# A one-layer transformer trunk in split float32: the gates of three paired blocks put behind the copies of their last sums, two embedding splits put behind the last pair's, and every queue ordered by the scheduler's timeline model

## The chip, the cores and the metric

The kernel runs on one core of a Trainium2 chip. The metric is the device time of one execution in microseconds (us). Three executions of the kernel before took 662.04, 662.87 and 664.4 us; the median, 662.87 us, is what the change is measured against. The profile shown below is of one further execution, which took 664.42 us.

A core has five engines that work side by side, each through a queue of its own in strict order: TensorE (PE, matmuls), VectorE (DVE), ScalarE (ACT), GpSimd (POOL) and SyncE (SP), which here issues nearly all transfers from memory. They wait for one another by semaphores. An instruction whose data is not there yet holds up everything behind it on its engine.

## The reference

The layer is an attention mixer, a layer norm, a gated MLP with a causal convolution, a second layer norm, and a gated embedding. Sequence 512, width 1024, 16 heads of 64, inner width 2816, all in float32:

```python
proj = x @ w_in                                  # q, k, v, f_logit
c = cumsum(log_sigmoid(f_logit + b_f))           # per head
s = q @ k.T * scale + c[:, None] - c[None, :]    # causal
o = softmax(s) @ v
x = layer_norm(ALPHA * x + o @ w_out, ln_mix_g, ln_mix_b)
u, g = split(x @ ffn_w_up)
g = causal_dwconv(g, conv_w, conv_b)             # 3 taps
x = layer_norm(ALPHA * x + (gelu(g) * u) @ ffn_w_down, ln_ffn_g, ln_ffn_b)
x = x + sigmoid(x @ ple_w_gate + ple_b_gate) * (p @ ple_w_proj)
```

## The kernel before

**Split products.** A float32 product is made of three matmuls in a faster format. Each operand is split into a high part (`xh`, `whi`), which ACT makes by a copy, and a low part (`xl`, `wlo`), which DVE makes by subtracting the high part from the original. `three` (L120) issues hi x hi, hi x lo and lo x hi into one PSUM bank. A matmul over 512 columns is the kernel's unit of work.

**Weights** come in units of 1024 columns (`Weights`): SP loads a unit into one of four buffers `raw`, ACT writes `whi` (L98), DVE writes `wlo` (L99), and a matmul reads both. Units are numbered in the order of use; `whi25` is the high part of unit 25. A unit's `home` gives it a tile of its own rather than one of the rotating five; only the embedding's splits (`moreh`, `morel`) have one.

**Stages.** Values (`pv`); then, for each of the 16 heads, projections for a pair of heads further on (`pp`, 24 matmuls each), scores (`s6_0` to `s6_3` are the four row blocks of head 6), softmax (DVE adds the mask, L404, and takes the negated maximum, L405; ACT takes the exponential with its sum, L406; POOL scales by the reciprocal, L414), ten transposes (`t`, L427) into three banks that ACT and DVE copy as high and low parts (`PTh`, L430, `PTl`, L431), and the product with the values (`o`, L440). The scores of a head are issued a head ahead of its transposes and two ahead of its values. Then the output projection (`ao` and `ap`, for the left and right 512 columns), the first layer norm, whose result is transposed back by PE (`nt`, L558) and split, the MLP's up products (`g` gate, `u` up) and down products (`x`, `y`, `z`), the last down products (`r`), the second layer norm, the embedding's product (`pl`), its gate (`gt`), and the output.

**A layer norm** here (`add_half`, `half_stats`, `norm`) costs DVE for each of four row tiles: two adds of a product (L533 or L535), two statistics (L540), an aggregate (L544), an addition (L545), then two passes over 1024 columns (L549 and L550), between which POOL raises to a power (L546). `flip` transposes the finished tile.

**Up pairs.** The inner blocks are worked in pairs. For pairs 4, 7 and 9 (`UP_PAIRS`) a scheme with fewer products is used, in four stages of sums (`up_step`); the sums end in `E4`, `E7` and `E9`. The last stage ends with a copy of a bank into E by ACT (L697). Then `conv_product` takes the gate through the convolution and Gelu (`conv`, `product`). Down products of the group of pairs before are issued in between, wherever `between()` stands.

**What sets the order.** The kernel is written in one thread; a scheduler (`TileContext`) places each instruction in its engine's queue by the priority that it had when written and by what is ready in the scheduler's own model. `BANKS` deals out the eight PSUM banks in turn. A new user of a bank waits for the last reader of the old one.

Of the kernel before, what the change touches and what calls it, by code (L numbers as in the profile page):

```python
# [12 lines left out]
AF = mybir.ActivationFunctionType  # L13
# [3 lines left out]
P = 128  # L17
S = 512
# [16 lines left out]
HALF = S // 2  # L35
# [21 lines left out]
class Weights:  # L57

    def __init__(self, nc, pool):
        self.nc, self.pool = nc, pool
        self.units, self.raw, self.parts = [], {}, {}
        self.loaded = self.cut = 0

# [19 lines left out]
    def cut_to(self, i):  # L85
        while self.cut < min(i, len(self.units)):
            self.load_to(self.cut + 1)
            _, n, _, make, home = self.units[self.cut]
            t = self.raw.pop(self.cut)
            if home is not None:  # L90
                hi, lo = home()
            else:
                hi, lo = [self.pool.tile([P, UNIT], F32R, tag=g, name=f"{g}{self.cut}", bufs=SPLIT_BUFS)
                          for g in ("whi", "wlo")]
            c = 0
            for piece in [t[:, :n]] if make is None else make(t):
                e = c + piece.shape[-1]
                self.nc.scalar.activation(hi[:, c:e], piece, AF.Copy)  # L98
                self.nc.vector.tensor_sub(lo[:, c:e], piece, hi[:, c:e].bitcast(F32))  # L99
                c = e  # L100
            self.parts[self.cut] = (hi, lo)
            self.cut += 1

# [7 lines left out]
def trunk_layer(ctx: ExitStack, tc: tile.TileContext, xT, x2d, pT, wqk, wv0, wv1, wv2, bf, wo, wup, cwb,  # L111
                wdn, wpl, wg, bg, gm, bm, gf, bff, out):
    nc = tc.nc
# [9 lines left out]
    base = ctx.enter_context(tc.tile_pool(name="base", bufs=1))  # L123
# [8 lines left out]
    def half_rows(w, k0, n, cols):  # L132
        return w[k0 * P:(k0 + n) * P, cols * 512:(cols + 1) * 512].rearrange("(k p) c -> p k c", p=P)

    W = Weights(nc, base)
    wv = (wv0, wv1, wv2)
    u_v, u_qk = {}, []

# [79 lines left out]
    for part in range(4):  # L218
# [3 lines left out]
        for i in range(2 * len(fs)):  # L222
            f, q = fs[i // 2], i % 2
# [13 lines left out]
                    u_up[j, 3, sq] = stages[3](sq)  # L237
        assert not todo
    u_r = [[W.add(half_rows(wdn, k, 2, n), inner=512) for k in REST[::2]] for n in range(2)]
    extra = []  # L240

    def apart(i):
        return lambda: [t[:, i] for t in extra]

    u_p = W.add(pT.rearrange("(k p) t -> p k t", p=P), inner=S, home=apart(0))
    u_pl = [W.add(half_rows(wpl, 0, 2, n), inner=512, home=apart(1 + n)) for n in range(2)]
# [410 lines left out]
    def up_step(j, st, s, E):  # L657

        if st == 0:
            ups[j, s] = bank(f"{'gu'[s]}{2 * j}", "two" if j > 2 else None)
        ps = ups[j, s]
        z, x = ps[:, :HALF], ps[:, HALF:]
        hi, lo = W.get(u_up[j, st, s], 2)
        first, second = slice(0, HALF), slice(HALF, S)

        def go(to, col, on, a=None, sn=None, last=4):
            for k in range(4):
                w = slice((4 * col + k) * P, (4 * col + k + 1) * P)  # L670
                if a is None:
                    mh, ml = [v[:, 4 * sn + k, :] for v in xs]
                else:
                    mh, ml = [v[:, a[0] + k, a[1]] for v in (x1h, x1l)]
                three(to, hi[:, w], lo[:, w], mh, ml, k == 0 and not on, k == 3, on=on)

        e = E[:, (1 - s) * 2 * S:(2 - s) * 2 * S]
        c1, c2 = side(5)[:, s * HALF:(s + 1) * HALF], side(6 + s)
        if st == 0:
            go(z, 1, False, a=(4, first))  # L680
            go(x, 0, True, a=(0, first))
            nc.scalar.activation(c1, z, AF.Copy)
            nc.scalar.activation(z.rearrange("p (a b) -> p a b", b=P),
                                 zeros.unsqueeze(1).to_broadcast([P, 2, P]), AF.Copy)
            nc.vector.tensor_add(e[:, :HALF], x, c1)
        elif st == 1:
            go(z, 0, True, sn=0)
            go(x, 1, True, sn=1)
            nc.scalar.activation(c2[:, :HALF], x, AF.Copy)
            nc.scalar.activation(c2[:, HALF:], z, AF.Copy)  # L690
        elif st == 2:
            go(z, 1, True, sn=3)
            go(x, 0, True, sn=2)
            nc.vector.tensor_add(e[:, S:], ps, c2)  # L694
        else:
            go(x, 0, True, a=(4, second))
            nc.scalar.activation(e[:, HALF:S], x, AF.Copy)  # L697
            del ups[j, s]

    def conv_product(f, E):  # L700

        c = slice(f % 2 * S, f % 2 * S + S)
        ups[f, 0], ups[f, 1] = E[:, 2 * S:][:, c], E[:, c]
        conv(f)
        product(f, E[:, c])
# [61 lines left out]
    for part in range(4):  # L767
        ops = []
        slots = iter(CHUNKS[part] or ())

        def between():
            for _ in range(next(slots, 0)):
                next(before)

        for f in range(6 * part, min(6 * part + 6, NF)):
            q, j = f % 2, f // 2
            if q == 0:
                E = hpool.tile([P, 8 * HALF], F32, tag="E", name=f"E{j}")
            if f == 0:
                a, b = slice(0, HALF), slice(HALF, S)  # L780
                up(0, 0, a)
                up(0, 1, a)
                up(1, 0, a, (3, x1h, x1l, xt))
                up(0, 0, b)
                up(0, 1, b)
                up(1, 0, b)
                conv(0)
                product(0, E[:, :S])
                continue
            if j in UP_PAIRS:  # L790
                if q == 0:
                    up_step(j, 0, 0, E)
                    between()
                    up_step(j, 0, 1, E)
                    between()
                    continue
                for st in (1, 2):
                    up_step(j, st, 0, E)
                    up_step(j, st, 1, E)
                    if st == 1:  # L800
                        between()
                conv_product(f, E)
                between()
                up_step(j, 3, 0, E)
                up_step(j, 3, 1, E)
                conv_product(f - 1, E)
            else:
                if f > 1:
                    up(f, 0)
                conv(f)  # L810
                between()
                up(f, 1)
                product(f, E[:, q * S:(q + 1) * S])
            if f == 1:
                x_sums()
            if q:
                if part < 3:
                    ops.append([cut_tiles("A", 2, 3, f"a{j}"), cut_tiles("B", 1, 5, f"b{j}", pool=hpool),
                                cut_tiles("S", 4, 4, f"s{j}")])
                    operands(ops[-1], E)  # L820
                else:
                    h, l = cut_tiles("S", 4, 4, f"s{j}")
                    e = E[:, :2 * S].rearrange("p (a b) -> p a b", b=HALF)
                    nc.scalar.activation(h, e, AF.Copy)
                    nc.vector.tensor_sub(l, e, h.bitcast(F32))
                    ops.append((h, l))
            if j not in UP_PAIRS:
                between()
        if part < 3:
            before = down(part, ops)  # L830
# [126 lines left out]
```

## Time and profile before

| | |
|---|---|
| three executions | 662.04, 662.87, 664.4 us |
| profiled execution | 664.42 us |
| its span (first to last instruction) | 662.7 us |
| PE busy | 650.9 us (98%) |
| DVE busy | 514.3 us (78%) |
| ACT busy | 339.2 us (51%) |
| POOL busy | 84.3 us (13%) |
| TensorE clock granted, mean | 0.996 |

Busy times of the engines overlap and are not to be added. In the rows of the timeline the columns are start, duration, engine, line, operation, result and sources, and how many instructions of that kind follow each other; in square brackets stands the idle time of the engine before the row and what ended it. Consecutive instructions of one engine overlap a little in these records (a DVE instruction starts some 0.08 us before the end of the one before it, a copy on ACT some 0.1 us), so a row of durations adds up to a little more than the time it takes.

### The profile page before, as it was taken

The page shows a single profiled execution, that of the slowest core. Times are in us where ns is not written, and L with a number is a line of the kernel's source. Part 1 is how long each engine was busy: PE and PEld are TensorE (multiplying, and loading weights), DVE is VectorE, ACT ScalarE, POOL GpSimd, SP SyncE. Part 2 cuts the span into 40 slices and gives each one's busy share as a digit, 9 for nine tenths or more (in the row PEclk, how much of TensorE's full clock was granted, in tenths as well). Part 3 has the DMA queues.
Part 4 walks back from the last instruction along what each step waited for, and adds up shares of the span by engine and source line. Part 5 has one row for each costly group of instructions (what it writes and reads, how often), then busy time and mean ns, then how long its engine had stood idle before and what let it go on. Part 6 is the DMA issues. An engine that isn't in the chain of part 4 may idle for free.

```text
span 662.7 us, 9314 instructions
## 1 busy us (share of the span) xinstructions
PE 650.9 (98%) x3450; PEld 563.4 (85%) x3450; DVE 514.3 (78%) x830; ACT 339.2 (51%) x589; POOL 84.3 (13%) x78
## 2 busy tenths in 40 slices
PE   8999999999999999999999999999999989999997
PEld 7899888888888889888889888889888978788886
DVE  7674789998886699954889696797878887599364
ACT  5644677787775255643445544354545543516231
POOL 0000554445445020000000000000000000011000
PEclk9999999999999999999999999999999989999999
DMA  8433122112262313433344554645544553651221
GB/s 291 158 129 128 64 66 66 42 57 66 65 227 107 120 43 101 133 117 95 102 139 145 181 156 146 182 131 191 185 137 126 186 157 120 203 204 64 71 79 48
DMA packets 35485, 83.29 MB, mean 126 GB/s; under 512 B 3248, under 2 KB 7088, under 8 KB 35440
## 3 DMA queue, kind: packets, MB, share of 16 engines
q1 hardware_dynamic: 35440, 82.70, 38.6%
q8 instruction: 27, 0.44, 0.3%
q14 instruction: 18, 0.15, 0.1%
HBM read 80.46 MB, written 2.10 MB: 125 GB/s over the span
## 4 chain that ended last, share of the span: by engine, by line
PE 88%; DMA 4%; DVE 4%; ACT 2%; issue 2%; SPq 0%; ACTq 0%; DVEq 0%
PE g L120 16%; PE u L120 15%; PE pp L120 13%; PE gt L120 7%; PE pv L120 6%; PE x L120 6%; PE ao L120 3%; PE ap L120 3%; PE o L440 3%; PE r L120 3%; PE z L120 3%; PE t L427 2%; DMA raw<-wdn 2%; DVE wlo L99 2%; PE pl L120 2%
## 5 line engine op out<-in xcount | busy, mean ns | idle before, releaser
L98 ACT ACTIVATE whi<-raw 128x1024 fp32r<-128x1024 f32 (+5 forms) x143 | 133.3, 934 | 136.7 <-PE g L120 44.4
L99 DVE TENSOR_TENSOR wlo<-raw,whi 128x1024 fp32r<-128x1024 f32 (+5 forms) x143 | 151.4, 1065 | 53.9 <-ACT whi L98 53.7
L414 POOL TENSOR_SCALAR pr<-pr,rl 128x128 f32<-128x128 f32 (+1 forms) x64 | 72.0, 1143 | 135.7 <-DVE rl L410 135.7
L120 PE MATMUL g<-x1h,whi 128*128 128x512 f32 (+1 forms) x180 | 64.0, 355 | 3.4 <-ACT E L697 3.4
L120 PE MATMUL g<-x1l,whi 128*128 128x512 f32 (+1 forms) x180 | 63.5, 353 | 0.0
L120 PE MATMUL g<-x1h,wlo 128*128 128x512 f32 (+1 forms) x180 | 63.4, 352 | 0.0
L120 PE MATMUL u<-x1h,whi 128*128 128x512 f32 (+1 forms) x172 | 61.5, 357 | 0.7 <-DVE E L694 0.7
L120 PE MATMUL u<-x1l,whi 128*128 128x512 f32 (+1 forms) x172 | 61.4, 357 | 0.0
L120 PE MATMUL u<-x1h,wlo 128*128 128x512 f32 (+1 forms) x172 | 61.4, 357 | 0.0
L546 POOL TENSOR_TENSOR mv<-mv,neghalf 128x1 f32<-128x1 f32 x8 | 11.6, 1447 | 386.5 <-DVE mv L545 364.2
L120 PE MATMUL pp<-xh,wlo 128*128 128x512 f32 x128 | 50.5, 395 | 0.0
L120 PE MATMUL pp<-xh,whi 128*128 128x512 f32 x128 | 50.0, 390 | 0.0
L120 PE MATMUL pp<-xl,whi 128*128 128x512 f32 x128 | 50.0, 390 | 0.0
L406 ACT ACTIVATE pr<-s,nm 128x128 f32<-128x128 f32 (+1 forms) x64 | 33.4, 526 | 17.4 <-DVE nm L405 14.3
L120 PEld LDWEIGHTS g<-x1h,whi 128*128 128x128 f32 x180 | 34.4, 191 | 8.6 <-ACT E L697 4.0
L120 PEld LDWEIGHTS g<-x1l,whi 128*128 128x128 f32 x180 | 34.4, 191 | 4.7
L120 PEld LDWEIGHTS g<-x1h,wlo 128*128 128x128 f32 x180 | 34.5, 191 | 4.6
L120 PEld LDWEIGHTS u<-x1h,whi 128*128 128x128 f32 x172 | 32.5, 189 | 5.6 <-issue 0.9
L120 PEld LDWEIGHTS u<-x1l,whi 128*128 128x128 f32 x172 | 32.5, 189 | 4.8
L120 PEld LDWEIGHTS u<-x1h,wlo 128*128 128x128 f32 x172 | 32.5, 189 | 4.7
L630 ACT ACTIVATE a<-a 128x512 f32<-128x512 f32 x22 | 13.9, 631 | 34.8 <-DVE a L628 34.8
L120 PE MATMUL pv<-whi,xh 128*128 128x384 f32 (+1 forms) x96 | 30.3, 328 | 1.0 <-ACT whi L98 1.0
(535 smaller groups left out, 1624.6 us busy)
## 6 DMA issues: line engine op xcount, KB each, us to landing
raw<-wup SPq DMA_DIRECT2D x50, 512.0 KB
raw<-wdn SPq DMA_DIRECT2D x31, 512.0 KB
raw<-wqk SPq DMA_DIRECT2D x16, 512.0 KB
raw<-wo SPq DMA_DIRECT2D x8, 512.0 KB
raw<-wg SPq DMA_DIRECT2D x8, 512.0 KB
raw<-wv SPq DMA_DIRECT2D x8, 384.0 KB
side<-wdn SPq DMA_DIRECT2D x9, 256.0 KB
raw<-wdn SPq DMA_DIRECT2D x9, 256.0 KB
```

Source lines behind the costliest of these rows:

```text
L98: self.nc.scalar.activation(hi[:, c:e], piece, AF.Copy)
L99: self.nc.vector.tensor_sub(lo[:, c:e], piece, hi[:, c:e].bitcast(F32))
L120: nc.tensor.matmul(ps, lhsT, rhs, start=start and n == 0, stop=stop and n == 2, skip_group_check=on)
L406: nc.scalar.activation(pr[:, off:off + w], ps[:, :w], AF.Exp, bias=nm[:, i:i + 1], accum_out=ls[:, i:i + 1])
L414: nc.gpsimd.tensor_scalar_mul(pr[:, off:off + w], pr[:, off:off + w], rl[:, i:i + 1])
L427: nc.tensor.transpose(ps[:, w:w + P], pr[:, o:o + P], ident)
L440: nc.tensor.matmul(ps[:, q0:], V[:, j, h], p[:, o:o + w], start=j == 0 and n == 0, stop=j == NT - 1 and n == 1)
L546: nc.gpsimd.tensor_tensor(mv[:, 3:4], mv[:, 2:3], neghalf, op=ALU.pow)
L630: nc.scalar.activation(a, a, AF.Gelu)
```

## The change

Four things are changed; no instruction is added or taken away on any engine, and no arithmetic is changed.

1. A unit with a `home` is split inside `issue_after(first)`, where `first` is the ACT copy that starts the last pair's splits (`s10h<-E10`, L824 before). The embedding's three splits (`moreh`, `morel`) so stand behind it in ACT's queue.
2. The copies and additions that end each stage of `up_step` are written under `tc.high_priority()`, and the last stage returns the ACT copy with which it ends.
3. In pairs 4, 7 and 9 both calls of `conv_product` stand after the last stage and inside `issue_after` of its copy. So the ACT work of the two gates stands behind the copy of the last sum.
4. `TileContext` is given `schedule_with_timeline_sim=True`: the scheduler orders all queues by another model of the engines' time.

```diff
             t = self.raw.pop(self.cut)
+            behind = ExitStack()
             if home is not None:
-                hi, lo = home()
+                hi, lo, first = home()
+                behind.enter_context(self.tc.issue_after(first))
...
+            behind.close()
             self.parts[self.cut] = (hi, lo)
...
-    extra = []
+    extra, last_cut = [], []
     def apart(i):
-        return lambda: [t[:, i] for t in extra]
+        return lambda: [t[:, i] for t in extra] + [last_cut[0]]
...
         if st == 0:
             go(z, 1, False, a=(4, first))
             go(x, 0, True, a=(0, first))
-            nc.scalar.activation(c1, z, AF.Copy)
-            nc.scalar.activation(z.rearrange("p (a b) -> p a b", b=P),
-                                 zeros.unsqueeze(1).to_broadcast([P, 2, P]), AF.Copy)
-            nc.vector.tensor_add(e[:, :HALF], x, c1)
+            with tc.high_priority():
+                nc.scalar.activation(c1, z, AF.Copy)
+                nc.scalar.activation(z.rearrange("p (a b) -> p a b", b=P),
+                                     zeros.unsqueeze(1).to_broadcast([P, 2, P]), AF.Copy)
+                nc.vector.tensor_add(e[:, :HALF], x, c1)
...
         else:
             go(x, 0, True, a=(4, second))
-            nc.scalar.activation(e[:, HALF:S], x, AF.Copy)
             del ups[j, s]
+            with tc.high_priority():
+                return nc.scalar.activation(e[:, HALF:S], x, AF.Copy)
...
-                conv_product(f, E)
                 between()
                 up_step(j, 3, 0, E)
-                up_step(j, 3, 1, E)
-                conv_product(f - 1, E)
+                with tc.issue_after(up_step(j, 3, 1, E).ins):
+                    conv_product(f, E)
+                    conv_product(f - 1, E)
...
-                    nc.scalar.activation(h, e, AF.Copy)
+                    last_cut[:] = [nc.scalar.activation(h, e, AF.Copy).ins]
...
-    with tile.TileContext(nc) as tc:
+    with tile.TileContext(nc, schedule_with_timeline_sim=True) as tc:
```

Parts 1 and 3 put instructions behind one that is named. Part 4 moves instructions everywhere, also in the attention and the layer norms, which parts 1 to 3 do not touch. Three places show it. In the changed file the lines stand two or three lower (L98 is L100, L431 is L434, L550 is L553).

**In the attention, at head 6.** ACT's queue from the copies of projection 3 on, before and then in the changed kernel (`t4_0`, `t4_1`, `t4_3` are the banks of head 4's transposes):

```order
L379 ACTIVATE KA6_1217<-pp3_1_1191 64x512
L380 ACTIVATE KB0_295<-pp3_1_1191 64x512
L430 ACTIVATE PTh0_299<-t4_0_1226 128x512
L430 ACTIVATE PTh0_299<-t4_1_1233 128x384
L430 ACTIVATE PTh0_299<-t4_3_1239 128x384
L379 ACTIVATE KA7_1259<-pp3_1_1191 64x512
L446 ACTIVATE o_1_1149<-o3_1245 64x512
L380 ACTIVATE KB1_296<-pp3_1_1191 64x512
L98 ACTIVATE whi25_1607<-raw25_1305 128x1024
```

```order
L382 ACTIVATE KA6_1217<-pp3_1_1191 64x512
L383 ACTIVATE KB0_295<-pp3_1_1191 64x512
L100 ACTIVATE whi25_1607<-raw25_1305 128x1024
L433 ACTIVATE PTh0_299<-t4_0_1226 128x512
L433 ACTIVATE PTh0_299<-t4_1_1233 128x384
L433 ACTIVATE PTh0_299<-t4_3_1239 128x384
L382 ACTIVATE KA7_1259<-pp3_1_1191 64x512
L383 ACTIVATE KB1_296<-pp3_1_1191 64x512
```

DVE's queue at the same place, before and then in the changed kernel:

```order
L383 TENSOR_TENSOR KA6_1217<-pp3_1_1191,KA6_1217 64x512
L431 TENSOR_TENSOR PTl0_301<-t4_0_1226,PTh0_299 128x512
L431 TENSOR_TENSOR PTl0_301<-t4_1_1233,PTh0_299 128x384
L431 TENSOR_TENSOR PTl0_301<-t4_3_1239,PTh0_299 128x384
L447 TENSOR_TENSOR o_1_1149<-o3_1245,o_1_1149 64x512
```

```order
L386 TENSOR_TENSOR KA6_1217<-pp3_1_1191,KA6_1217 64x512
L101 TENSOR_TENSOR wlo25_1608<-raw25_1305,whi25_1607 128x1024
L434 TENSOR_TENSOR PTl0_301<-t4_0_1226,PTh0_299 128x512
L407 TENSOR_TENSOR s6_0_1271<-s6_0_1271,mask_82 128x128
L407 TENSOR_TENSOR s6_1_1272<-s6_1_1272,mask_82 128x128
L434 TENSOR_TENSOR PTl0_301<-t4_1_1233,PTh0_299 128x384
L407 TENSOR_TENSOR s6_2_1277<-s6_2_1277,mask_82 128x128
L434 TENSOR_TENSOR PTl0_301<-t4_3_1239,PTh0_299 128x384
```

The two halves of the split of unit 25 have moved ahead of the copies of the transposes, and three mask additions stand between those copies.

**In the first layer norm.** DVE's queue, before and then in the changed kernel (`ap0`, `ap1`, `ap2` are the right half products of row tiles 0, 1 and 2; `mv_2505` belongs to tile 0, `mv_2538` to tile 1):

```order
L533 SCALAR_TENSOR_TENSOR y_2210<-y_2210,ap0_2454 128x512
L540 BN_STATS st0_2443<-y_2210 128x6
L544 BN_AGGR mv_2505<-st0_2443 128x2
L545 TENSOR_SCALAR mv_2505<-mv_2505 128x1
L549 SCALAR_TENSOR_TENSOR y_2210<-y_2210,mv_2505,g1_2426 128x1024
L550 SCALAR_TENSOR_TENSOR y_2210<-y_2210,mv_2505,b1_2428 128x1024
L533 SCALAR_TENSOR_TENSOR y_2210<-y_2210,ap1_2511 128x512
```

```order
L536 SCALAR_TENSOR_TENSOR y_2210<-y_2210,ap2_2544 128x512
L547 BN_AGGR mv_2538<-st1_2446 128x2
L548 TENSOR_SCALAR mv_2505<-mv_2505 128x1
L552 SCALAR_TENSOR_TENSOR y_2210<-y_2210,mv_2505,g1_2426 128x1024
L543 BN_STATS st2_2449<-y_2210 128x6
L548 TENSOR_SCALAR mv_2538<-mv_2538 128x1
L552 SCALAR_TENSOR_TENSOR y_2210<-y_2210,mv_2538,g1_2426 128x1024
L553 SCALAR_TENSOR_TENSOR y_2210<-y_2210,mv_2505,b1_2428 128x1024
```

PE's queue where the transposes of tile 0 stand, before and then in the changed kernel:

```order
L120 MATMUL ap2_2544<-whi34_2455,ol_98 128x512
L120 MATMUL ap2_2544<-wlo34_2456,oh_97 128x512
L558 MATMUL nt_2557<-ident_80,y_2210 128x128 x4
L558 MATMUL nt_2564<-ident_80,y_2210 128x128 x4
L120 MATMUL ap2_2544<-whi35_2467,oh_97 128x512
```

```order
L123 MATMUL ap2_2544<-whi36_2479,ol_98 128x512
L123 MATMUL ap2_2544<-wlo36_2480,oh_97 128x512
L561 MATMUL nt_2557<-ident_80,y_2210 128x128 x4
L561 MATMUL nt_2564<-ident_80,y_2210 128x128 x4
L123 MATMUL ap3_2593<-whi33_2371,oh_97 128x512
```

Tile 0 was finished on DVE before the product `ap1` was read; now its last pass stands seven rows behind the reading of `ap2`, and its transposes on PE follow the last matmul of `ap2` at once.

**In the second layer norm.** DVE's queue up to the last pass of the third tile (`mv_5654`), before and then in the changed kernel:

```order
L549 SCALAR_TENSOR_TENSOR y_2210<-y_2210,mv_5654,g2b2_5518 128x1024
L535 TENSOR_TENSOR y_2210<-y_2210,r1_0_5674 128x512
L550 SCALAR_TENSOR_TENSOR y_2210<-y_2210,mv_5654,g2b2_5518 128x1024
L540 BN_STATS st1_5688<-y_2210 128x6
L535 TENSOR_TENSOR y_2210<-y_2210,r1_1_5690 128x512
```

```order
L101 TENSOR_TENSOR wlo137_5807<-raw137_5583,whi137_5806 128x1024
L538 TENSOR_TENSOR y_2210<-y_2210,r1_0_5674 128x512
L101 TENSOR_TENSOR wlo138_5819<-raw138_5585,whi138_5818 128x1024
L548 TENSOR_SCALAR mv_5654<-mv_5654 128x1
L552 SCALAR_TENSOR_TENSOR y_2210<-y_2210,mv_5654,g2b2_5518 128x1024
L101 TENSOR_TENSOR wlo139_5831<-raw139_5777,whi139_5830 128x1024
L538 TENSOR_TENSOR y_2210<-y_2210,r1_1_5690 128x512
L101 TENSOR_TENSOR wlo140_5843<-raw140_5810,whi140_5842 128x1024
L543 BN_STATS st1_5688<-y_2210 128x6
L566 TENSOR_TENSOR x2l_5522<-nt_5711,x2h_5521 128x4x128
L566 TENSOR_TENSOR x2l_5522<-nt_5718,x2h_5521 128x4x128
L553 SCALAR_TENSOR_TENSOR y_2210<-y_2210,mv_5654,g2b2_5518 128x1024
```

Four splits of the gate's weights (`wlo137` to `wlo140`), an addition, a statistic and the two halves of `x2l` now stand ahead of that last pass, which they followed before. The transposes that read it stand, before and now, at the same row of PE's queue, directly behind the product `pl1_0`.

More of the change, by code (lines that the diff above doesn't have):

```diff
@@ L57, with __init__ @@
 class Weights:
-    def __init__(self, nc, pool):
-        self.nc, self.pool = nc, pool
+    def __init__(self, tc, pool):
+        self.tc, self.nc, self.pool = tc, tc.nc, pool
         self.units, self.raw, self.parts = [], {}, {}
@@ L133, in half_rows @@
         return w[k0 * P:(k0 + n) * P, cols * 512:(cols + 1) * 512].rearrange("(k p) c -> p k c", p=P)
-    W = Weights(nc, base)
+    W = Weights(tc, base)
     wv = (wv0, wv1, wv2)
@@ L688, in up_step @@
             go(x, 1, True, sn=1)
-            nc.scalar.activation(c2[:, :HALF], x, AF.Copy)
-            nc.scalar.activation(c2[:, HALF:], z, AF.Copy)
+            with tc.high_priority():
+                nc.scalar.activation(c2[:, :HALF], x, AF.Copy)
+                nc.scalar.activation(c2[:, HALF:], z, AF.Copy)
         elif st == 2:
@@ L693, in up_step @@
             go(x, 0, True, sn=2)
-            nc.vector.tensor_add(e[:, S:], ps, c2)
+            with tc.high_priority():
+                nc.vector.tensor_add(e[:, S:], ps, c2)
         else:
             go(x, 0, True, a=(4, second))
-            nc.scalar.activation(e[:, HALF:S], x, AF.Copy)
             del ups[j, s]
+            with tc.high_priority():
+                return nc.scalar.activation(e[:, HALF:S], x, AF.Copy)
     def conv_product(f, E):
```

## Prediction

> **What bounds the kernel now.** I read the page first, then PE's waits, then the chain of waits, then the timeline at the places that the change reorders.
>
> ```profile
> span 662.7 us, 9314 instructions
> PE 650.9 (98%) x3450; PEld 563.4 (85%) x3450; DVE 514.3 (78%) x830; ACT 339.2 (51%) x589; POOL 84.3 (13%) x78
> PEclk9999999999999999999999999999999989999999
> ```
>
> PE is busy for 650.9 of 662.7 us, so the end is set by PE's own work and by what makes it stand still. Little can be won, and whatever makes PE wait is added to the end in full. The one 8 in the clock's row is the slice from 530 to 547 us. PE's waits (engine, line, what it waited for: us in total, times, the longest):
>
> ```profile
> PE g L120 <- ACT E L697: 3.4, 3, 1.8
> PE r L120 <- ACT s10h L824: 1.6, 1, 1.6
> PE u L120 <- DVE E L694: 0.7, 1, 0.7
> ```
>
> These five waits, 5.7 us together, are the three up pairs and the last products. From the chain of waits two groups of 24 matmuls of one kind, and from the timeline what stands around the second:
>
> ```profile
> 394.70 5.44 PE g L120 x24
> ...
> 540.64 7.36 PE g L120 x24
> ...
> 537.19 0.36 PE L120 MATMUL u<-x1h,whi 128*128 128x256 f32 x1 [0.72 <-DVE E L694]
> 540.64 0.50 PE L120 MATMUL g<-x1h,whi 128*128 128x512 f32 x1 [1.78 <-ACT E L697]
> 541.83 0.63 PE L120 MATMUL g<-x1l,whi 128*128 128x512 f32 x1
> 542.25 0.63 PE L120 MATMUL g<-x1h,wlo 128*128 128x512 f32 x1
> ```
>
> 5.44 us is 227 ns a matmul. The group at 540.64 took 1.92 us more: some of its matmuls started 0.42 us apart (541.83 to 542.25) in the slice of the lower clock, behind waits of 0.72 and 1.78 us within 4.4 us. A fall of the granted clock costs about 1.9 us here.
>
> Whether other stages have room is read from the windows (columns: window, its length, busy us and instructions of PE, PEld, DVE, ACT, POOL, then clock, DMA share, GB/s):
>
> ```profile
> 120.00:160.00 40.00, 40.00 (x218) 34.31 (x217) 36.16 (x77) 30.58 (x75) 17.23 (x17) 1.00 0.18 54
> ...
> 580.00:600.00 20.00, 20.00 (x93) 16.44 (x92) 19.80 (x31) 4.96 (x7) 4.07 (x3) 1.00 0.48 167
> ```
>
> In the attention PE never stops, but DVE is busy 90% and ACT 76% of the time: 1 us a head is left for steps that come late. In the second norm DVE has no room at all.
>
> **What the change saves.** All waits quoted above lose their reason. Behind each pair's last sum down products (12 matmuls in pairs 4 and 7, more in pair 9) now stand ahead of the next gate: at 227 ns 2.7 us of work, against waits of at most 1.8. Of `r`, 22 matmuls instead of 6 stand ahead of the first that reads `s10h` (3.6 us more cover against 1.6), and `s10h` no longer stands behind `moreh`. With the clock that stays up: -(5.7 + 1.9) = **-7.6 us**. It is a gain at its best; nothing is removed, so less than nothing can't be saved either.
>
> **What the reordering costs in the attention.** Before, at head 6 (timeline: start, duration):
>
> ```profile
> 113.88 0.58 ACT L380 ACTIVATE KB<-pp 64x512 fp32r<-64x512 f32 x1
> 114.36 1.34 ACT L430 ACTIVATE PTh<-t 128x512 fp32r<-128x512 f32 x3
> 117.32 1.05 ACT L98 ACTIVATE whi<-raw 128x1024 fp32r<-128x1024 f32 x1
> ...
> 111.51 1.21 DVE L99 TENSOR_TENSOR wlo<-raw,whi 128x1024 fp32r<-128x1024 f32 x1
> 115.21 1.62 DVE L431 TENSOR_TENSOR PTl<-t,PTh 128x512 fp32r<-128x512 f32 x3
> 118.30 0.50 DVE L404 TENSOR_TENSOR s<-s,mask 128x128 f32<-128x128 f32 x2
> ...
> 113.19 1.25 PE L427 MATMUL t<-ident,pr 128*128 128x128 f32 x10
> 116.47 0.56 PE L398 MATMUL s<-KB,QB 68*128 68x384 f32 x2
> ```
>
> The third `PTl` ended at 116.83; PE's next projection, which takes that bank, followed the scores' end at 117.03, 0.2 us to spare. Now `whi25` stands ahead of `PTh` on ACT and `wlo25` ahead of `PTl` on DVE, with three masks between the three `PTl`. On the old clock: `KB0` ends at 114.46, `whi25` at 115.5, `wlo25` 1.2 us later at 116.7; three `PTl` (1.62) and three masks (3 x 0.25) end at 119.1. PE has only three more transposes ahead of the projection (0.3 us, 117.4). So PE waits 119.1 - 117.4 = 1.7 us. This order stands at heads 6, 10 and 14.
>
> At heads 8 and 12 the fourth block of scores (`s8_3`) is moved behind a whole projection, 24 x 227 ns = 5.4 us later. Its softmax then runs in a row: mask, `wlo28` (now ahead of the maximum), maximum, exponential:
>
> ```profile
> L99 DVE TENSOR_TENSOR wlo<-raw,whi 128x1024 fp32r<-128x1024 f32 x99 | 120.3, 1218 | 41.9 <-ACT whi L98 41.8
> L404 DVE TENSOR_TENSOR s<-s,mask 128x128 f32<-128x128 f32 x64 | 15.6, 289 | 3.5 <-PE s L398 3.3
> L405 DVE TENSOR_REDUCE nm<-s 128x1 f32<-128x512 f32 x16 | 10.8, 678 | 0.0
> L406 ACT ACTIVATE pr<-s,nm 128x512 f32<-128x512 f32 x16 | 11.0, 689 | 0.0
> L406 ACT ACTIVATION_READ_ACCUMULATOR pr<-s,nm 128x1 f32 x64 | 12.5, 195 | 0.0
> ```
>
> 0.29 + 1.22 + 0.68 + 0.69 + 0.19 = 3.1 us, 3.9 with a wait behind copies on ACT; PE has some 2.5 us of work (eight matmuls of `o`, the transposes, four scores) before it needs that bank for `s9_2`. That is 0.6 to 1.4 us; I take 1.3, since two `PTh` copies do stand ahead of that exponential. The two heads between have a split ahead of their copies too, with more work for PE between: 1.0 each, bounds 0 and the 1.7 above. A round of four heads then loses 1.7 + 1.0 + 1.0 + 1.3 = 5.0 us, and heads 3 to 14 are three rounds: **+15 us**, bounds 6 (only the three places at 1.7 and half of the two at 1.3) and 20 (1.7 at all twelve).
>
> At the attention's end the scores of head 15 stand one projection's length later, so the output product `ao` follows 0.55 us behind `o13`, whose result still goes ACT, DVE, ACT (about 0.6 each by the copies above): 1.8 - 0.55 = 1.3, and 0.5 at the last transposes: **+1.8**, bounds 0.5 and 2.8.
>
> **In the first norm.** Before, DVE and then PE:
>
> ```profile
> 231.02 0.21 DVE L544 BATCH_NORM_AGGREGATE mv<-st 128x2 f32<-128x12 f32 x1
> 231.26 0.15 DVE L545 TENSOR_SCALAR mv<-mv 128x1 f32<-128x1 f32 x1
> 231.33 1.28 DVE L549 SCALAR_TENSOR_TENSOR y<-y,mv,g 128x1024 f32<-128x1024 f32 x1
> 233.07 1.28 DVE L550 SCALAR_TENSOR_TENSOR y<-y,mv,b 128x1024 f32<-128x1024 f32 x1 [0.46 <-POOL mv L546]
> 234.27 0.68 DVE L533 SCALAR_TENSOR_TENSOR y<-y,ap 128x512 f32<-128x512 f32 x1
> 234.99 0.69 DVE L540 BATCH_NORM_STATS2 st<-y 128x6 f32<-128x512 f32 x1
> ...
> 236.44 1.03 PE L558 MATMUL nt<-ident,y 128*128 128x128 f32 x8
> ```
>
> Tile 0 was done at 234.35 and its transposes came at 236.44: 2.1 us to spare. Now they follow the last matmul of `ap2`, and DVE, which waits for that matmul first, still has to do the addition 0.68, 0.21, 0.15, a pass 1.28, a statistic 0.69, 0.15, a pass of the other tile 1.28, and tile 0's last pass 1.28: 5.7, less 0.07 overlap for each of seven, 5.2 us, with nothing on PE in between. **+5.2**, bounds 4.7 and 5.7. What follows (`x1h` to the first `g`) is closer by a copy: **+0.9**, bounds 0 and 1.
>
> **In the second norm.** Before:
>
> ```profile
> 579.45 1.23 DVE L825 TENSOR_TENSOR s10l<-E,s10h 128x1024 fp32r<-128x1024 f32 x1
> ...
> 600.41 1.28 DVE L550 SCALAR_TENSOR_TENSOR y<-y,mv,g2b 128x1024 f32<-128x1024 f32 x1
> 602.21 0.67 DVE L535 TENSOR_TENSOR y<-y,r 128x512 f32<-128x512 f32 x1
> 602.80 0.68 DVE L563 TENSOR_TENSOR x2l<-nt,x2h 128x512 fp32r<-128x512 f32 x1
> ...
> 607.36 1.03 PE L558 MATMUL nt<-ident,y 128*128 128x128 f32 x8
> ```
>
> The third tile was done at 601.69, its transposes came at 607.36: 5.7 us to spare. DVE's queue between `s10l` and that pass now holds on balance three splits more, and two of `morel`, which the change put behind `s10h`: five at 1.15 us, and three additions, statistics or halves of `x2l` at 0.6, 7.5 us together. PE arrives 1.6 us earlier, since the wait at `r` is gone. 7.5 + 1.6 - 5.7 = **+3.4**, bounds 1.4 (if DVE's own gaps take some) and 3.8.
>
> **In pair 9** an addition that frees a bank of `x` now stands behind a split of 1.23 us and two instructions that wait for transfers: **+1.5**, bounds 0 and 2.5; a like place in pair 7 **+0.4**, bounds 0 and 0.4.
>
> **The clock.** Waits of this size can bring the half clock, at 1.9 us each time: the one at 540 us came behind 2.5 us of standing still in 4.4. The first norm (5.2) and the second (3.4) are beyond that: **+3.8**, bounds 0 and 7.7 (four such places). [...]
>
> **Sum:** -7.6 + 15 + 1.8 + 5.2 + 0.9 + 3.4 + 1.5 + 0.4 + 3.8 = +24.4 us. On the profiled execution (664.42 us: the span of 662.7 and 1.7 around it) that is 688.8; it stands 1.55 above the median, so on the median **687.3**, 3.7% slower. All bounds low give +5 (668), all high +36 (699).
>
> **The rivals.** A change within 0.3% (2 us) can't be told from none.
>
> First, faster. The down products cover the pairs' waits and the new orders are covered as well, because PE's queue starts late enough everywhere: 662.87 - 7.6 = 655.3. For it speaks that the saved waits are real rows; against it that the first norm alone has 5.2 us with nothing on PE. It decides as soon as all new waits together stay under 7.6 us. 4%.
>
> Second, the attention absorbs its reordering: after one late copy all later steps are late alike, and PE's projections of 5.4 us catch up. Then 2 us instead of 15 and one fall of the clock: 662.87 + 24.4 - 13 - 1.9 = 672.4. For it speaks PE's 40.00 of 40.00; against it DVE's 36.16, which leaves 1 us a head to catch up. 12%.
>
> Third, the clock also falls inside the attention, where waits of 1 to 2 us come every few us: at one fall a head, 8 to 10 times 1.9 us less what the waits hide, about +13: 700. Against it: a wait of 1.3 us at 378 us was followed by 24 matmuls in 5.76, not 7.36.
>
> ```profile
> 379.42 5.76 PE g L120 x24
> ```
>
> 9%. Fourth, the flag changes less on the chip than in the queues, and all comes out within 2 us: 2%. The forecast keeps 73%. Range **672 to 699**; faster 4%, the same 2%, slower 94%.
>
> **What would show it.** In the changed profile: no wait of `g` for `E` and of `r` for `s10h`; PE waits for `PTl` and `pr` between 88 and 215 us, 10 to 20 us in all; one wait of about 5 us of `nt` for the first norm's last pass, and one of 3 for the second's; a PEclk below 9 near the first norm. It is wrong if PE keeps 40.00 of 40 in the attention, or if the transposes of tile 0 come without a wait.

## The result, and the profile after

| | before | changed |
|---|---|---|
| median of 4 executions each, alternating | 663.63 us (662.04 to 665.12) | 698.17 us (697.62 to 698.97) |
| profiled execution | 664.42 us | 697.62 us |
| its span | 662.7 us | 695.9 us |
| PE busy | 650.9 us (98%) | 661.1 us (95%) |
| granted clock, mean | 0.996 | 0.986 |

The ratio is 1.0522, 95% interval 1.0492 to 1.0551: the changed kernel is 5.2% slower. The forecast was 687.3, with a range of 672 to 699; the direction was right, the time lies at the range's upper edge, and the likeliest value was 11 us too low; 0.8 of that is the median of the kernel before, 663.63 here and 662.87 when the forecast was made.

From the page of the changed kernel, busy times by engine, PE's share in each of 40 slices, and the clock's:

```profile
PE 661.1 (95%) x3450; PEld 566.3 (81%) x3450; DVE 517.2 (74%) x830; ACT 338.9 (49%) x589; POOL 84.9 (12%) x78
PE   8999979898899896999999999999999999998997
PEclk9999999999999998999999999999999999999999
```

PE's row shows where the time went: in the first 16 slices (up to 278 us), that is in the attention and the first norm, and once more near the end. PE's waits in the changed kernel (engine, line, what it waited for: us in total, times, the longest):

```profile
PE nt L561 <- DVE y L553: 8.6, 3, 5.2
PE pp L123 <- DVE PTl L434: 4.9, 6, 1.2
PE s L399 <- DVE PTl L434: 3.2, 4, 1.0
PE s L399 <- ACT pr L409: 2.9, 3, 1.3
PE s L399 <- DVE o L450: 2.0, 3, 1.5
...
PE x L123 <- DVE y L538: 1.5, 1, 1.5
...
PE ao L123 <- ACT oh L452: 1.3, 1, 1.3
```

All waits of before are gone: no row has `g` or `u` waiting for `E`, or `r` for `s10h`. In their place stand, from 30 us on, 31 waits of more than 0.1 us with 27.6 us of idle time, where before had 6 with 5.9 us (the last line above, 1.3, is the attention's end). Two stretches, with columns as in the prediction (busy us and instructions of PE, PEld, DVE, ACT, POOL, then clock, DMA share, GB/s):

```profile
85.00:214.00 129.00, 113.84 (x577) 92.66 (x576) 99.26 (x207) 82.86 (x196) 53.39 (x48) 0.97 0.17 55
...
120.00:160.00 40.00, 34.68 (x184) 28.24 (x183) 31.20 (x64) 27.00 (x63) 13.66 (x13) 1.00 0.17 54
```

From 120 to 160 us PE now runs 34.68 us of 40, where it ran all 40.00. DVE, which has the same work to do in the attention as a whole, fell from 36.16 to 31.20 in this stretch: both now wait for each other.

To compare kernels by stretch I use PE's *loss*: over all matmuls of a stretch, the time from one start to the next, less what that step takes for the same two kinds of matmul when nothing disturbs it. It holds the idle time, what a wait costs beyond it, and stretches of half clock. It depends a little on which steps are called undisturbed; taking them from the kernel of experiment 1 moves the attention's figures by up to 0.8 us. The stretches are those of each kernel's own span; the words say what the changed kernel does there, and the one before is ahead of it by up to 33 us.

| PE's loss, us (stretch) | before | changed |
|---|---|---|
| attention (85 to 214) | 2.3 | 25.1 |
| attention's end (214 to 250) | 0.2 | 4.7 |
| output projection, first norm (250 to 300) | 0.0 | 8.6 |
| pairs (300 to 500) | 2.1 | 0.0 |
| pairs (500 to 560) | 4.7 | 1.8 |
| from 560 to the end | 2.1 | 3.8 |

With the start, which barely differs, the whole span has 14.4 and 47.3 us of loss: 32.9 us of the 33.2 by which the spans differ.

### The profile page after: what moved, and what is told of

Its sections match the earlier page's. It is cut to its first block, busy times and chain, and to the rows that moved or that the text cites. A ratio compares the mean times of both kernels' runs of the same rounds, so it can differ in the third digit from the quotient of the medians.

```text
span 695.9 us, 9366 instructions
## 1 busy us (share of the span) xinstructions
PE 661.1 (95%) x3450; PEld 566.3 (81%) x3450; DVE 517.2 (74%) x830; ACT 338.9 (49%) x589; POOL 84.9 (12%) x78
## 4 chain that ended last, share of the span: by engine, by line
PE 78%; DVE 12%; ACT 3%; DMA 3%; issue 2%; SPq 0%; DVEq 0%; ACTq 0%
PE g L123 15%; PE u L123 15%; PE pp L123 13%; PE gt L123 6%; PE pv L123 6%; PE x L123 6%; PE ap L123 3%; DVE wlo L101 3%; PE ao L123 3%; PE z L123 3%; PE r L123 2%; ACT whi L100 2%; DVE PTl L434 2%; DMA raw<-wup 1%; DVE y L538 1%
## 5 line engine op out<-in xcount | busy, mean ns | idle before, releaser
L100 ACT ACTIVATE whi<-raw 128x1024 fp32r<-128x1024 f32 (+5 forms) x143 | 132.9, 933 | 134.5 <-PE g L123 50.0
L123 PE MATMUL pp<-xh,wlo 128*128 128x512 f32 x128 | 52.2, 408 | 5.2 <-DVE PTl L434 4.9
L123 PE MATMUL pp<-xl,whi 128*128 128x512 f32 x128 | 51.6, 403 | 0.0
L123 PEld LDWEIGHTS pp<-xh,wlo 128*128 128x128 f32 x128 | 24.8, 194 | 13.1 <-DVE PTl L434 5.6
```

The costliest lines, as they stand in the source:

```text
L123: nc.tensor.matmul(ps, lhsT, rhs, start=start and n == 0, stop=stop and n == 2, skip_group_check=on)
```

## The experiments

Ten kernels, each timed alternately with the kernel before on the same chip; "before" below is that comparison's own median. Line numbers in their rows are those of each kernel's own text. Unless said otherwise a kernel computes everything.

**1. Parts 1 to 3 without the flag.** The new way of ordering is left out, the three edits stay.

```diff
-    with tile.TileContext(nc, schedule_with_timeline_sim=True) as tc:
+    with tile.TileContext(nc) as tc:
```

> Parts 1 to 3 alone, the scheduler's old model for all queues. Theory (all of the loss is the reordering of part 4, and parts 1 to 3 save what was forecast): PE has none of the waits of g for E and of r for s10h, 85 to 300 us looks as before, 654 to 658 us. Rival (parts 1 to 3 cost something themselves, as the gates now stand late and hold up E and the down products): 662 us or more, with new PE waits in the three pairs.

Measured: 657.68 against 662.81, ratio 0.9924 (0.9903 to 0.9945). The one wait of PE that is left in the pairs (its span is 654.9 us):

```profile
PE u L123 <- DVE E L700: 1.1, 1, 1.1
```

The three `g` waits and the `r` wait are gone, as forecast; the wait of `u` stayed and is longer than before (1.1 against 0.7). Parts 1 to 3 save 5.1 us, and the flag costs 40 us on top of them.

**2. The flag alone**, on the kernel before.

```diff
-    with tile.TileContext(nc) as tc:
+    with tile.TileContext(nc, schedule_with_timeline_sim=True) as tc:
```

> Part 4 alone. Theory: the attention loses the same 22 to 23 us, its end 4 to 5, the first norm 5 to 6 and a fall of the clock: 692 to 699 us in all. The old waits of g for E go too, if the new order alone puts down products in front of the gates; then parts 1 to 3 were not needed for it. Rival (the loss needs parts 1 to 3 as well): under 685 us.

Measured: 695.65 against 662.81, ratio 1.0517 (1.0483 to 1.0551). Two of its waits:

```profile
PE nt L558 <- DVE y L550: 8.6, 2, 5.2
...
PE s L396 <- DVE PTl L431: 3.2, 4, 1.0
```

The whole loss is the flag's, with the same rows as in the changed kernel but one: the 1.5 us of `x` in pair 9 are absent here. Nor does any `g` wait for `E` here: the new order takes the pairs' waits away by itself, so under the flag parts 1 to 3 have nothing left to save. The second norm's wait is here too, with 3.4 us (8.6 less 5.2), though part 1 is absent.

**3. The old order in the attention and the first norm.** The changed kernel, but from the first score of head 0 to the end of the first norm each engine is held to the order of the kernel of experiment 1, by pairs of neighbours in that order (`ORDER`: instruction numbers by engine).

```diff
+def pin(tc):
+    at = {i.name: i for i in tc.nc.cur_bb.bb.instructions}
+    for ids in ORDER.values():
+        for a, b in zip(ids, ids[1:]):
+            tc.add_manual_dep(at[f"I-{b}"], f"I-{a}", mybir.DependencyInfo(
+                mybir.DependencyClass.NoSync, mybir.DependencyReason.DATA), reason="pin")
...
         trunk_layer(tc, *args)
+        pin(tc)
```

> The changed kernel, with the instructions of the attention and the first norm (PE, DVE, ACT, POOL) held in the order that they had before. Theory: between 85 and 300 us PE loses 2 to 3 us instead of 38.4, so 661 to 665 us; the wait of x for y (1.7) and the two of nt for the second norm (3.8) stay. Rival (part of the loss is not the order of these stages but comes from the transfers or from elsewhere): 670 us or more.

Measured: 661.32 against 662.81, ratio 0.9968 (0.9956 to 0.998). Of the flag's 40 us, 3.6 are left (against 657.68 in experiment 1). Window of the attention, and PE's timeline in the second norm (start, duration, in brackets the idle time before):

```profile
85.00:214.00 129.00, 128.78 (x703) 110.78 (x702) 113.67 (x240) 95.78 (x228) 62.58 (x56) 1.00 0.26 87
```

```profile
603.58 1.09 PE L561 MATMUL nt<-ident,y 128*128 128x128 f32 x8 [2.63 <-DVE y L553]
...
604.82 0.63 PE L123 MATMUL pl<-moreh,morel 128*128 128x512 f32 x1
605.25 0.63 PE L123 MATMUL pl<-morel,moreh 128*128 128x512 f32 x1
```

With the old order PE runs through again, and the loss in the attention is back at 2.3 us. What is left is mostly the second norm's wait, behind which the clock fell in this execution (0.89 from 595 to 610 us): matmuls start 0.43 us apart.

**4. The old order on DVE, ACT and POOL only, in the attention.** As experiment 3, but `ORDER` ends at the last matmul of `ao`'s tiles and has no list for PE, which keeps its new order.

> The changed kernel, with DVE, ACT and POOL held in the old order in the attention alone; PE keeps its new order. Theory (the splits ahead of the copies of the transposes on ACT and DVE make most of the loss, the moved score matmuls on PE the rest): 15 to 10 us less than the changed kernel, 682 to 688; the waits of pp and t for PTl go, waits of s stay at heads 4, 8, 9, 12 and 13. Rival (PE's own order makes the loss): 694 us or more.

Measured: 684.45 against 662.81, ratio 1.0303 (1.0269 to 1.0337).

**5. The old order on PE only, in the attention.** The other way round: `ORDER` has PE's list alone, over the same stretch.

> The changed kernel with PE alone held in the old order in the attention; DVE, ACT and POOL keep the new one. Theory (the order on ACT and DVE makes most of the loss): no gain to speak of, 693 to 700 us, with waits of pp and s for PTl throughout. Rival (PE's moved score matmuls make it): 685 us or less.

Measured: 693.48 against 663.52, ratio 1.0454 (1.0408 to 1.05). The largest waits of PE in the attention, experiment 4 first:

```profile
PE s L399 <- DVE KA L386: 5.5, 3, 2.4
```

```profile
PE s L399 <- DVE PTl L434: 8.9, 9, 1.6
```

PE's loss in the attention, by whose order is new:

| | PE old | PE new |
|---|---|---|
| DVE, ACT, POOL old | 2.3 (experiment 3) | 10.4 (experiment 4) |
| DVE, ACT, POOL new | 25.9 (experiment 5) | 25.1 (changed kernel) |

The new order of the other engines alone brings the whole loss, whichever order PE has; PE's own new order costs 8 us when the others are as before, most of it by scores that reach the keys (`KA`) too early (5.5 us of idle time; 2.1 more are scores that wait for `PTl`). The profiled execution of experiment 4 took 679.62 us, 4.8 less than its median, so the 8 us may be more in others. The two orders don't add: where DVE is late, PE's new order costs nothing more. At the attention's end it is PE's order that counts: 4.2 us of loss with it (experiment 4), 1.5 without (experiment 5).

**6. Three of the twelve places alone.** Parts 1 to 3 without the flag, and at heads 6, 10 and 14 ACT's and DVE's rows held as the changed kernel has them: the split ahead of the three copies on ACT and on DVE, with the masks between the copies. Pairs of instructions as in experiment 3; the pairs of head 6 on DVE are, in the order held:

```
wlo25, PTl0 (t4_0), mask s6_0, mask s6_1, PTl0 (t4_1), mask s6_2, PTl0 (t4_3), o_1, KA7
```

> Parts 1 to 3 with the old model, and only the order on ACT and DVE at heads 6, 10 and 14 as the changed kernel has it (units 25, 29 and 33 split ahead of the copies of the transposes, three masks between the low halves). Theory: at each of the three places PE waits 1.6 to 1.9 us for PTl, as in the changed kernel (1.21 + 0.38 + 0.31 at 123 us): 4.8 to 5.7 us over parts 1 to 3 alone, 662 to 664 us. Rival (in the old surroundings the softmax has the room to take the split in): under 1 us, 658.5 or less.

Measured: 662.39 against 663.71, ratio 0.9977 (0.9959 to 0.9996). The scores wait for `PTl` three times, 2.5 us in all. PE at head 6:

```profile
117.02 0.50 PE L399 MATMUL s<-KA,QA 128*128 128x512 f32 x1 [0.75 <-DVE PTl L434]
...
117.97 0.63 PE L430 MATMUL t<-ident,pr 128*128 128x128 f32 x4 [0.22 <-DVE PTl L434]
```

PE's loss in the attention is 7.1 us against 2.3 in experiment 1: 4.8 us for three places, 1.6 each, against 1.7 in the prediction. So this order (a split of 1.2 us ahead of the copies, masks between them) is a cause by itself.

**7. The first norm's new order alone.** Parts 1 to 3 without the flag; of the new order only DVE's rows between `ap2` and the last pass of tile 0, written out by hand, with the transposes of tiles 0 and 1 placed to match.

```diff
-            if t > 1 and k == 3:
-                flip(t - 2, x1h, x1l, xt)
+            if t == 3 and k == 5:
+                flip(1, x1h, x1l, xt)
...
+        read = add_half(t, 1, ps, True)
+        if t == 2:
+            with tc.issue_after(read):
+                first = norm(0, g1, b1, defer=True)
+                half_stats(2, 1)
+                second = norm(1, g1, b1, defer=True)
+                first()
+                flip(0, x1h, x1l, xt)
+                second()
...
```

(`defer` makes `norm` give back its last pass instead of issuing it; `add_half` gives back its instruction.)

> Parts 1 to 3 with the old model, and only the first norm's DVE order of the changed kernel: the passes of tiles 0 and 1 behind the reading of ap2, tile 0's transposes behind that. Theory: one wait of nt for y of 5.2 to 5.6 us, up to 1.3 more at x1l and g, and one fall of the clock behind it (1.4 to 1.9): 7 to 9 us over parts 1 to 3 alone (657.7), 664 to 667 us. Rival (the wait belongs to the attention's lateness, not to this order): under 660 us.

Measured: 664.7 against 663.52, ratio 1.0018 (0.9993 to 1.0042), so all that parts 1 to 3 save is lost again. Its wait and the window around it:

```profile
PE nt L568 <- DVE y L556: 5.3, 1, 5.3
```

```profile
238.00:252.00 14.00, 8.68 (x37) 7.12 (x36) 12.45 (x18) 5.16 (x7) 4.00 (x3) 0.76 0.04 10
```

The wait is the one predicted, to 0.1 us, and the clock fell behind it (0.76 in the window). From 214 to 250 us PE's loss is 7.8 us, where experiment 1 has 0.2: 5.3 idle, and the rest nearly all half clock.

**8. Part 1 alone**, and **9. parts 2 and 3 alone**, both without the flag. In 9 the line `behind.enter_context(self.tc.issue_after(first))` is left out; in 8 `conv_product` stands where it stood, without `issue_after`, and nothing is written under `high_priority`.

> Part 1 alone (the embedding's splits behind the copy s10h), old model. Theory: only the wait of r for s10h (1.6 us, 1.8 with its tail) goes; the waits of g and u for E and the fall of the clock at 540 us stay: 660.5 to 662 us. Rival (the freed time is given back in the second norm, whose DVE work now starts later): 662.5 us or more, with a wait of nt for y.

> Parts 2 and 3 alone (stage ends first, gates behind the last sum), old model. Theory: the three waits of g for E (3.4 us) and the fall of the clock (1.6 to 1.9) go, the wait of u for E (0.7 to 1.3) and that of r for s10h stay: 657.5 to 659.5 us. Rival (the gain of parts 1 to 3 comes mostly from part 1): 661 us or more.

Measured: part 1 alone 662.62 against 663.52, ratio 0.9978 (0.9951 to 1.0006); parts 2 and 3 alone 659.24 against 663.52, ratio 0.9929 (0.9904 to 0.9954). Waits of the one, then of the other:

```profile
PE g L123 <- ACT E L705: 3.8, 3, 1.8
```

```profile
PE u L122 <- DVE E L699: 1.6, 1, 1.6
...
PE r L122 <- ACT s10h L830: 1.0, 1, 1.0
```

Each edit takes away its own wait and leaves the other's. Parts 2 and 3 bring 4.3 us, as expected. Part 1 alone lies just above its expected range, with no wait of `nt` for `y` as the rival would have it; whether it brings anything this can't tell.

**10. The last wait of the pairs taken away.** Parts 1 to 3 without the flag, and one pair of instructions turned round. Experiment 1 left `u` waiting for DVE's `E`. DVE there and then here (start, duration):

```profile
532.27 0.69 DVE L188 TENSOR_TENSOR raw<-raw 128x512 f32<-128x512 f32 x1 [1.74 <-DMA raw<-wdn]
532.88 1.22 DVE L101 TENSOR_TENSOR wlo<-raw,whi 128x1024 fp32r<-128x1024 f32 x1
534.02 0.68 DVE L700 TENSOR_TENSOR E<-u,side 128x512 f32<-128x512 f32 x1
```

```profile
532.07 0.68 DVE L700 TENSOR_TENSOR E<-u,side 128x512 f32<-128x512 f32 x1
532.67 0.68 DVE L188 TENSOR_TENSOR raw<-raw 128x512 f32<-128x512 f32 x1
```

In experiment 1 DVE stood 1.74 us at a subtraction on a weight unit that had not arrived, and the sum that frees PE's bank stood behind it and a split. The edit puts the subtraction behind the sum (the split, whose data are there, stays ahead of it):

```diff
+        tc.add_manual_dep(at["I-5280"], "I-5197", mybir.DependencyInfo(
+            mybir.DependencyClass.NoSync, mybir.DependencyReason.DATA), reason="behind the last sum")
```

> Parts 1 to 3 with the old model, and one DVE addition that waits for a transfer (L188, unit 121) put behind the last pair's addition of u18 (L700). Theory: the wait of u for E (1.1 to 1.3 us) goes and at most 0.4 comes back at g20: 656.5 to 657.5 us. Rival (the split of unit 121 is then late for the down products): 658 us or more.

Measured: 656.6 against 663.71, ratio 0.9886 (0.9863 to 0.991); the `u` wait is gone, and 0.3 us of a wait of `g` for `E` has come in its place. It is the fastest of all versions run, and faster than both kernels. Its six times lie within 1.0 us and those of experiment 1 within 3.9; since the two were timed in different comparisons and their intervals touch, the gain of this step by itself is likely, not shown.

## Why the prediction was right, and some 9 us short

The prediction's sum was +24.4 us; the spans differ by 33.2 (the medians by 34.5). In the terms of the loss, of which the two profiles differ by 32.9 us:

| | forecast | measured |
|---|---|---|
| waits taken away (idle) | -5.7 | -5.9 |
| new waits (idle) | +28.2 | +27.6 |
| cost of each wait beyond its idle time | none | +6.5 (31 x 0.26 less 6 x 0.26, below) |
| clock (two falls forecast in place of one; four came), and the rest | +1.9 | +4.7 |
| sum | +24.4 | +32.9 |

**The new waits** came almost term by term, as sums:

| term | forecast | idle measured |
|---|---|---|
| attention | 15 | 15.25 |
| attention's end | 1.8 | 1.78 |
| first norm | 5.2 | 5.25 |
| `x1h` to the first `g` | 0.9 | 0.25 |
| second norm | 3.4 | 3.37 |
| `x` in pair 9 | 1.5 | 1.54 |
| pair 7 | 0.4 | 0 |

That is closer than its bounds deserve, and two rows owe part of it to luck. In the second norm the reason was partly wrong (below). In the attention heads 6, 10 and 14 brought 1.41, 1.13 and 0.99 us of idle time, not 1.7 each, and PE waits where the prediction names nothing: 1.5 us in all for the keys (`KA`) and 1.5 for `o` at 102 us. The mechanism at head 6 is as told: ACT, DVE and PE in the changed kernel there.

```profile
121.59 1.05 ACT L100 ACTIVATE whi<-raw 128x1024 fp32r<-128x1024 f32 x1
122.54 1.33 ACT L433 ACTIVATE PTh<-t 128x512 fp32r<-128x512 f32 x3
```

```profile
122.68 1.50 DVE L101 TENSOR_TENSOR wlo<-raw,whi 128x1024 fp32r<-128x1024 f32 x1 [0.27 <-ACT whi L100]
124.10 0.68 DVE L434 TENSOR_TENSOR PTl<-t,PTh 128x512 fp32r<-128x512 f32 x1
```

```profile
123.28 0.34 PE L399 MATMUL s<-KA,QA 128*128 128x384 f32 x1
123.45 0.33 PE L401 MATMUL s<-KB,QB 68*128 68x384 f32 x1
124.83 0.50 PE L399 MATMUL s<-KA,QA 128*128 128x512 f32 x1 [1.05 <-DVE PTl L434]
...
125.78 0.52 PE L430 MATMUL t<-ident,pr 128*128 128x128 f32 x3 [0.22 <-DVE PTl L434]
```

The split runs first on ACT and then on DVE, which is done with it at 124.18; the first `PTl` follows, and PE stands until it has freed the bank. The prediction had one wait at the projection; there are three smaller ones, 1.05, 0.22 and, at the projection, 0.14 us: 1.41 idle and 1.9 lost against 1.7. At heads 8 to 9 the moved block of scores brought 1.33 and 0.22, against 1.3.

**The step that failed: a wait was priced at its idle time alone.** In the rows above the step from 123.45 to 124.83 takes 1.38 us, where a step behind a matmul of as many columns takes 0.17 undisturbed (123.28 to 123.45): 1.21 lost, 0.16 more than the 1.05 of idle. The rows also say where the 0.16 comes from. Matmuls overlap in these records, whose ends the profile models: the one at 123.45 lasts 0.33 us, though undisturbed the next would start 0.17 behind it. The idle time is counted from the end of the record, so a wait loses this overlap on top of it. It is therefore the same at other lengths: 0.22 of idle at 158.35 us lost 0.39, and the 5.25 of the first norm lost 5.40. The step behind the wait is often longer too. In the kernel before, behind the wait of 1.78 that ended at 540.64, the next two matmuls are these:

```profile
540.98 0.39 PE L120 MATMUL g<-x1l,whi 128*128 128x512 f32 x1
541.21 0.39 PE L120 MATMUL g<-x1h,wlo 128*128 128x512 f32 x1
```

From 540.64 to 540.98 are 0.34 us, where the step behind takes the usual 0.23. Over the 31 waits the lost overlap is 0.18 us on the average (0.16, or 0.24 behind a transpose) and the longer step 0.08 (0.03 to 0.13, without one that the half clock lengthened): 0.26 a wait. That is 8.1 us for 31 waits and 1.6 for the 6 of before, together the +6.5 that the sum lacks. The profile of before showed it already: the wait of 0.72 at 537.19 us cost 0.88. I read the idle time in brackets and stopped there; a change that trades few waits for many short ones is mispriced by just this.

**The clock** was under-counted, and at other places than thought. Windows of the changed kernel, PE's timeline at the first of them, and then a window with no fall:

```profile
100.00:107.00 7.00, 5.06 (x16) 3.52 (x16) 6.84 (x16) 5.03 (x13) 4.26 (x4) 0.76 0.23 76
...
201.00:207.00 6.00, 5.78 (x17) 4.28 (x18) 5.76 (x14) 2.57 (x9) 4.06 (x4) 0.72 0.13 48
239.00:243.00 4.00, 2.94 (x10) 2.45 (x10) 1.04 (x2) 1.18 (x3) 0.75 (x1) 0.63 0.15 61
272.00:278.00 6.00, 5.83 (x19) 5.01 (x20) 5.55 (x9) 3.33 (x5) 1.45 (x1) 0.53 0.00 0
...
630.00:645.00 15.00, 12.34 (x63) 10.09 (x62) 14.89 (x21) 7.68 (x12) 4.04 (x2) 1.00 0.40 114
```

```profile
102.11 0.50 PE L399 MATMUL s<-KA,QA 128*128 128x512 f32 x1 [1.54 <-DVE o L450]
...
103.25 0.51 PE L123 MATMUL pp<-xh,wlo 128*128 128x512 f32 x1 [0.40 <-DVE PTl L434]
103.56 0.63 PE L123 MATMUL pp<-xl,whi 128*128 128x512 f32 x1
103.99 0.63 PE L123 MATMUL pp<-xh,whi 128*128 128x512 f32 x1
```

The clock fell four times before PE's last matmul: twice in the attention, at its end, and behind the first norm; each of the first three halved it for 3.4 us (0.72 over 6 us), some eight matmuls at 0.43 us, and lost 1.6 to 1.8 us. Behind the first norm it was halved for 5.6 of the 6 us of the window (0.53), and some 2.6 us were lost. Behind the second norm, where I counted one, it stayed at 1.00 though PE had stood 2.66 us at a stretch. The third rival (falls inside the attention) was thus half right: two, not the eight to ten that it needed for its +13. The other rivals are refuted by the same rows: the attention didn't absorb its reordering (15 us idle, not 2), and the flag did change on the chip what it changes in the queues.

**The second norm** came out at 3.4, but part of its account is wrong. The sum counted five splits in DVE's queue behind `s10l`, two `morel` among them, as if DVE had never stood idle there. In the changed kernel it had caught up when the first product `r` was ready:

```profile
616.46 0.69 DVE L538 TENSOR_TENSOR y<-y,r 128x512 f32<-128x512 f32 x1 [1.07 <-PE r L123]
```

So what stands ahead of this addition, the `morel` included, cost nothing; with the flag alone, where part 1 is absent, DVE stood idle for 2.21 us at the same place. What counts stands behind it. From this addition to the end of the third tile's last pass (640.33) DVE needs 23.9 us, where it needed 19.4 before (582.33 to 601.69): 4.5 more, for four splits instead of two, and one addition, one statistic and two halves of `x2l` more. Why the wait is as long (3.4) with the flag alone, where both queues differ again, I did not resolve. In the changed kernel it comes in two pieces, the first tile's, which the prediction did not have, and the third's; that they add up to the forecast is luck:

```profile
624.84 1.09 PE L561 MATMUL nt<-ident,y 128*128 128x128 f32 x8 [0.71 <-DVE y L553]
...
640.39 1.09 PE L561 MATMUL nt<-ident,y 128*128 128x128 f32 x8 [2.66 <-DVE y L553]
```

**What the change saves** was credited to the wrong part. The waits did go, but under the flag they go without parts 1 to 3 (experiment 2); and without the flag these save 5.1 us of the 7.6. `u` keeps its wait until experiment 10 turns one more pair round. And the 1.9 of the clock is not to be had in every execution: of the 18 of the kernel before that were timed beside experiment 1, half had a mean granted clock of 0.999 or 1.0, against 0.996 in the profiled one.

**The first norm**, term by term: PE ends `ap2` and stands until DVE has done what the prediction lists.

```profile
267.70 1.27 DVE L552 SCALAR_TENSOR_TENSOR y<-y,mv,g 128x1024 f32<-128x1024 f32 x1
...
269.55 1.27 DVE L552 SCALAR_TENSOR_TENSOR y<-y,mv,g 128x1024 f32<-128x1024 f32 x1
```

```profile
266.54 0.39 PE L123 MATMUL ap<-wlo,oh 128*128 128x512 f32 x1
272.17 1.94 PE L561 MATMUL nt<-ident,y 128*128 128x128 f32 x8 [5.25 <-DVE y L553]
```

Between tile 0's first pass (267.70) and its last stand a statistic and the other tile's pass (269.55); nothing on PE covers them.

Why the timeline model chooses these orders, these runs don't tell. They show that its orders cost 5% on the chip, most of it on ACT and DVE in the attention, where a split stands ahead of a copy that PE waits for.

## What to carry to other kernels

Where PE is 98% busy, price a new wait at its idle time plus some 0.26 us (as measured here), and count how many waits there will be: many short ones cost more than the idle time says (here 8.1 us over 31 waits). A change of how *all* queues are ordered is to be tried apart from the local edits beside it: here those were worth 5 us, and 7 with one more pair turned round, and the flag hid them under 40. Ahead of an instruction that frees a PE bank nothing should stand that could run later: not a split of 1.2 us (three such places cost 4.8 us in experiment 6), and not one that waits for a transfer (1.74 us in experiment 1).

## What the runs showed of the hardware that was not expected

In these traces a wait of PE cost more than its idle time: some 0.16 us of overlap with the matmul before (0.24 behind a transpose), at 0.22 us of idle time as at 5.25, and up to 0.13 us at the next step.

The granted clock fell on less idle time than the 2.5 us in 4.4 that I had taken from the profile of before, and like waits had unlike outcomes: 1.33 and 0.22 us of idle time brought a fall at 201 us and none at 157 us, and a wait of some 2.6 us in the second norm brought one in experiment 3 (0.89 from 595 to 610 us) and none in the changed kernel (1.00 from 630 to 645 us). The falls of the changed kernel begin at 103.54, 202.53, 240.07 and 270.79 us; the first three last 3.41 us each and the fourth 6.83, at a clock of 0.50. In the 3.41 us that end at each of them PE's idle time adds up to 1.94, 1.55, 1.78 and 3.41 us, and to 1.78 in the kernel before (at 541.48; the 0.72 that the prediction counted with it lies further back). But in the 3.41 us that end at 158.35 us it is 1.55 as well, and in those that end at 640.39, in the second norm, 2.66, and neither brought a fall. So this sum alone doesn't decide it; what else does I leave open.
